# A two-layer hybrid decoder on one core: attention in another order, evacuations of one product put off, some transposes later

## The chip, the cores and the metric

The kernel runs on one core of one Trainium2 chip. The metric is the device time of one execution in microseconds. A core has a matrix engine (PE, with its weight loads shown apart as PEld), a vector engine (DVE), an activation engine (ACT), a general engine (POOL, GpSimd) and a queue engine (SP) that issues most of the transfers here. Each engine takes its own instructions in order, and they meet through semaphores.

## The reference, cut to what matters

One sequence of 1024 tokens, 1024 wide, goes through two layers in float32. Layer 0 mixes tokens with a gated linear recurrence (HGRN2, 8 heads of 128), layer 1 with sliding-window attention (window 128, 16 query heads of 64, 4 key/value heads, a learned sink per head and a shared relative-position bias). Each layer ends in a gated FFN with a causal convolution of width 3, and every sub-layer is `x <- LayerNorm(alpha * x + sublayer(x))`. The attention, which the change rewrites most, is

```python
logits = einsum('bntgrd,bnsgd->bngrts', q, kk) * scale + bias      # query block n against key blocks n-1, n
logits = where(mask, logits, -inf)                                 # 0 <= t - s < 128
m = maximum(logits.max(-1), sink)
p = exp(logits - m[..., None])
denom = p.sum(-1) + exp(sink - m)
o = einsum('bngrts,bnsgd->bntgrd', p, vv) / denom
```

Of the 256 keys that a query block sees, row t uses exactly 128: keys s > t of the block before and keys s <= t of its own block. The kernel therefore folds both halves into one 128 x 128 tile of probabilities per head and block.

## The kernel before, in words

**Precision.** A float32 product is made of three matmuls on high and low parts (`mm3`, L190 to L194): `split` writes the high part with an ACT copy (L218, a CAST) and the low part with a DVE subtraction (`low_part`, L166). A low part can be put off: when `split` gets a list, the subtraction is appended to it and runs when `make_lows` (L1376) empties the list. Smaller products run as plain float32 matmuls (`mm32`, L197) and transposes go through PE (`tr`, L201).

**Stages.** HGRN2 (to about 510 us), its output projection and the first FFN (to about 1230 us), keys and values, attention (about 1275 to 1470 us), the second output projection and FFN (to the end). The order on PE is the program's everywhere. In HGRN2 and in attention the orders on ACT, DVE and POOL are the program's too (`manual_schedule`); in the FFN stages DVE and ACT follow a planner.

**HGRN2.** A small planner, `Order`, interleaves the recurrence of one head with the projections of the next: `od.t` counts PE's estimated time, and a generator that yields a delay goes on when that time has passed. `norm` (L979) squares the head's output on ACT, takes the root on POOL, scales `og` on DVE (L990), yields `od.behind(0.5, 2.4)`, and then turns `og` by eight PE transposes.

**Output projection and normed rows.** `out_proj` (L299) makes the second half of the rows in the order of row blocks 4 to 7 and 0 to 3. For each, `Up.ln` (L360) normalises the row block on DVE (`ln_affine`: L249, L252), yields 8.0 us of PE time, and then turns the block on PE (L201) for the FFN.

**The FFN's second product.** `Down.product` (L600) computes seven products of the Strassen-Winograd form in the order 1, 2, 5, 6, 7, 3, 4. Each fills four PSUM banks (row blocks tb = 0 to 3); products 1, 5, 7 and 4 use the four banks of `psmm`, products 2, 6 and 3 those of two `psax` tiles, where tb = 0 and tb = 2 are the two halves of one tile, tb = 1 and tb = 3 those of the other. The last five blocks of the sum run bank after bank, and each bank is evacuated (`evacuate`, L582: L589 and L591 on DVE) as soon as its last matmul is issued. Product 3 of the last layer alone holds the evacuation of a bank back until the bank two later is done.

**Attention.** 32 iterations: c = 0 to 7 (a pair of head groups and a head within), bp = 0 to 3 (two query blocks). `attend` (L1279) is a generator with seven steps, and four iterations are in flight. Counted from the iteration n in which a unit starts:

| step | work | engine | in iteration |
|---|---|---|---|
| 1 | scores (L1290), copy of the own block's half to X (L1293) | PE, ACT | n |
| 2 | the other half by predicate (L1297), bias (L1303) | DVE, POOL | n |
| 3 | maximum (L1308, L1311), four exponentials with sums (L1315), the sink's (L1317) | DVE, ACT | n+1 |
| 4 | sum, reciprocal, scaling of X (L1319 to L1321) | DVE | n+1 |
| 5 | four transposes of X into one PSUM bank (L201) | PE | n+2 |
| 6 | two masked multiplications from that bank into W, s <= t and s > t (L1329) | DVE | n+2 |
| 7 | products with V of this block and the one before (L197), copy of the result (L1342) | PE, ACT | n+3 |

The loop (L1408 on) takes one step of each unit in flight: step 1 of the new one, 7 of the oldest, 3, 2, 5, 6, one filler on PE, 4, the split of a finished half of the next q (`q_split`, L1274 on ACT and L1276 on DVE, in every second iteration, bp = 0 and 2), the low parts that wait, and a second filler. A filler is six matmuls of 512 columns: of the next q's projection while c < 7, of the output projection (`out_part`) in c = 7. In the iterations 26 to 31 (`moves`) a finished piece of the attention's result is split into T (`Y_to_T`), its ACT cast at the head of the iteration. After the loop the last three units are taken to their ends by hand, with parts of the output projection between.

Of the kernel before, what the change touches and what calls it, by code (L numbers as in the profile page):

```python
# [10 lines left out]
F32 = mybir.dt.float32  # L11
# [24 lines left out]
def constant_arrays():  # L36
    s = np.arange(P)[:, None]
    t = np.arange(P)[None, :]
    masks = np.zeros((P, 7 * BL + P), np.float32)
    bs, bt = s % BL, np.arange(BL)[None, :]  # L40
    pair = lambda m: (bs // (2 * m) == bt // (2 * m)) & (bs % (2 * m) < m) & (bt % (2 * m) >= m)
    parts = [bs == bt, pair(1), pair(2) & (bs % 4 == 0), pair(2) & (bs % 4 == 1)] + [pair(1 << i) for i in range(2, 5)]
    for i, part in enumerate(parts):
        masks[:, i * BL:(i + 1) * BL] = part
    masks[:, 7 * BL:] = t > s
    tri = np.zeros((P, 2, P), np.float32)
    tri[:, 0] = s <= t
    tri[:, 1] = s > t
# [59 lines left out]
def trunk(ctx: ExitStack, tc: tile.TileContext, a: dict, out: bass.AP):  # L108
# [237 lines left out]
    class Up:  # L346
# [13 lines left out]
        def ln(self, tb):  # L360
            with urgent():
                ln_affine(tb, self.rows, lambda hs: ynd[:, tb, hs], 2 if tb == 3 else 1)
            yield 8.0
            turned = lambda t: (self.rx[2 * t - 4] if t in (2, 3) else Y[:, t, :]).rearrange("p (k t) -> p k t", k=KC)
# [145 lines left out]
    class Down:  # L510
# [89 lines left out]
        def product(self, i, ln):  # L600
# [7 lines left out]
            for k, tb in steps + [(k, tb) for tb in range(4) for k in range(late, H)]:  # L608
# [6 lines left out]
                if k == H - 1:  # L615
                    if i < 2:
                        self.later.append(lambda p=p, tb=tb: self.evacuate(p, tb, banks[tb], ln))
                    elif self.last and p == 3:
                        held.append(tb)
# [30 lines left out]
    with tc.tile_pool(name="t", bufs=1, reuse_waits="tile") as raws, hgrn_pool as hp:  # L650
# [328 lines left out]
        def norm(h, pv, og):  # L979
# [11 lines left out]
            od.vec(1.2)  # L991
            yield od.behind(0.5, 2.4)
            ps = psax()
# [198 lines left out]
    with (tc.tile_pool(name="ta", bufs=1, reuse_waits="tile") as raws,  # L1192
          tc.tile_pool(name="at", bufs=1, reuse_waits="tile") as at):
        raw_tail(raws)
        Kh = at.tile([P, 2, 2, S], F32R, name="Kh")
        tri = at.tile([P, 2, P], F32, name="tri")
        nc.scalar.dma_start(tri, a["tri"])
# [4 lines left out]
        Kl = at.tile([P, 2, S], F32R, name="Kl")  # L1202
        Vt = at.tile([P, NB, 256], F32, name="Vt")
        khl, uv = [], []
        for c in range(2):
# [23 lines left out]
        def v_part(tp):  # L1229
            ps = psmm()  # L1230
            proj_tok(uv, tp, ps)
            nc.scalar.copy(Vt[:, 2 * tp:2 * tp + 2, :], ps.rearrange("p (a b) -> p a b", a=2))

        wq = a["swa_w_q"][0].rearrange("(kc p) (h e) -> p kc h e", p=P, e=64)

        W0 = at.tile([P, 2, 4, P], F32, name="W0")
        bfs = {}
# [41 lines left out]
        def attend(c, bp, q):  # L1279
# [44 lines left out]
            for i in range(4):  # L1324
                tr(pt[:, i * P:(i + 1) * P], X[:, i // 2, i % 2, :])
            yield
            W = W0 if bp % 2 else Y[:, NB - 1, :].rearrange("p (k g s) -> p k g s", k=2, g=4)
            for k in range(2):
                nc.vector.tensor_tensor(W[:, k], pt.rearrange("p (g s) -> p g s", g=4),  # L1329
                                        tri[:, k, :].unsqueeze(1).to_broadcast([P, 4, P]), op=ALU.mult)  # L1330
            yield
            po = psmm()
            for jj in range(2):
                j = 2 * bp + jj
                for e in range(2):
                    kvc = (2 * pp + e) * 64
                    o = po[64 * e:64 * e + 64, jj * P:(jj + 1) * P]
                    mm32(o, Vt[:, j, kvc:kvc + 64], W[:, 0, 2 * e + jj, :], stop=j == 0)
                    if j:
                        mm32(o, Vt[:, j - 1, kvc:kvc + 64], W[:, 1, 2 * e + jj, :], start=False)  # L1340
            if c < 7:
                nc.scalar.copy(Y[:, c, bp * 256:(bp + 1) * 256], po[:, :256])  # L1342
            else:
                ts = slice(bp * 256, (bp + 1) * 256)
                split(T[:, 0, c, ts], T[:, 1, c, ts], po[:, :256], lows)
            yield
# [34 lines left out]
        with tc.manual_schedule(engines={EN.PE, EN.Activation, EN.DVE, EN.Pool}):  # L1381
# [117 lines left out]
```

## Time and profile before

| | |
|---|---|
| median of 3 runs | 2189.2 us (2187.97 to 2191.01) |
| the profiled execution's own time | 2192.32 us |
| span of the profile | 2190.5 us |
| PE busy / its weight loads | 99% / 83% of the span |
| DVE busy | 80% |
| ACT busy | 41% |
| POOL busy | 5% |
| granted TensorE clock, mean | 0.997 |

A busy PE is one with a matmul in flight; the ends of matmuls are modelled, so that short waits between two of them do not show as idle time, and a matmul at a lower clock counts as busy for longer. The two places to look are therefore the waits of PE and the granted clock. A row of a timeline gives the start in us, the length in us, engine, line, operation, out<-in, shapes and count, and in brackets how long the engine was idle before it and what ended that. A row of the windows gives for each engine the busy time and the number of instructions, then the granted clock, the share of the DMA engines and GB/s.

### The profile page before, as it was taken

To read this page: it belongs to the slowest core of one execution; us is meant where nothing else is said; L and a number is where in the kernel's file an instruction comes from. 1 tells how busy PE (TensorE), PEld (TensorE's weight loads), DVE (VectorE), ACT (ScalarE), POOL (GpSimd) and SP (SyncE) were. 2 spreads that over 40 slices of the span, in tenths; PEclk is the share of its full clock that TensorE was granted. 3 is DMA by queue.
4 is the path that set the end of the run, shared out by engine and by line. 5 is a ranking of instruction groups with operands and counts; after the bars stand their busy time and mean duration, and the time that the engine had idled before them with its cause. 6 is when DMAs were issued, how large, how long until landed. Compare 5 with 4: busy or idle time off the path is not lost.

```text
span 2190.5 us, 33214 instructions
## 1 busy us (share of the span) xinstructions
PE 2168.1 (99%) x13188; PEld 1813.6 (83%) x13188; DVE 1762.2 (80%) x2388; ACT 895.3 (41%) x1457; POOL 120.3 (5%) x135
## 2 busy tenths in 40 slices
PE   9999999999999999999999999999999999999998
PEld 8888888998888888888878888878888888888877
DVE  3776666667999988887978568969999988878986
ACT  3233333343444444444433256743544444434430
POOL 1000000000100000000001123211000000000001
PEclk9999999999999999999999999999999999999999
DMA  5654533305223222228854411133223222249662
GB/s 196 231 167 162 183 136 102 97 22 175 98 73 106 87 85 79 77 96 271 281 183 154 126 32 28 32 106 110 93 96 97 77 87 77 84 138 325 229 209 88
DMA packets 229844, 279.05 MB, mean 127 GB/s; under 512 B 29960, under 2 KB 158648, under 8 KB 226872
## 3 DMA queue, kind: packets, MB, share of 16 engines
q1 hardware_dynamic: 228736, 276.53, 38.7%
q8 instruction: 104, 1.70, 0.3%
q14 instruction: 52, 0.43, 0.1%
q10 hardware_dynamic: 856, 0.37, 0.1%
q0 software_dynamic: 96, 0.02, 0.0%
HBM read 213.94 MB, written 62.94 MB: 126 GB/s over the span
## 4 chain that ended last, share of the span: by engine, by line
PE 84%; DVE 9%; DMA 3%; issue 2%; ACT 2%; SPq 0%; POOL 0%; DVEq 0%; ACTq 0%; POOLq 0%
PE psmm L191 18%; PE psmm L193 17%; PE psmm L192 17%; PE psax L191 8%; PE psax L192 8%; PE psax L193 8%; PE psax L197 3%; DVE T L166 2%; PE psax L201 1%; DVE HL L166 1%; PE psmm L201 1%; PE psmm L197 1%; PE psax L1290 1%; DMA R<-bsd 1%; DMA rx<-gd 1%
## 5 line engine op out<-in xcount | busy, mean ns | idle before, releaser
L191 PE MATMUL psmm<-T,HL 128*128 128x512 f32 x768 | 307.4, 400 | 0.0
L192 PE MATMUL psmm<-T,HL 128*128 128x512 f32 x768 | 300.3, 391 | 0.0
L193 PE MATMUL psmm<-T,HL 128*128 128x512 f32 x768 | 300.2, 391 | 0.0
L470 DVE SCALAR_TENSOR_TENSOR Y<-Y,cwt 128x1023 f32<-128x1023 f32 (+1 forms) x176 | 225.1, 1281 | 43.3 <-ACT Y L468 39.9
L218 ACT CAST HL<-rx 128x1024 fp32r<-128x1024 f32 (+1 forms) x151 | 151.0, 1004 | 219.9 <-PE psmm L192 45.0
L191 PE MATMUL psmm<-HL,T 128*128 128x256 f32 (+1 forms) x656 | 198.3, 302 | 0.0
L193 PE MATMUL psmm<-HL,T 128*128 128x256 f32 (+1 forms) x656 | 194.3, 296 | 1.4 <-DVE T L166 1.4
L192 PE MATMUL psmm<-HL,T 128*128 128x256 f32 (+1 forms) x656 | 194.0, 296 | 0.0
L166 DVE TENSOR_TENSOR HL<-rx,HL 128x1024 fp32r<-128x1024 f32 (+1 forms) x151 | 174.4, 1161 | 19.1 <-ACT HL L218 18.9
L193 PEld LDWEIGHTS psmm<-T,HL 128*128 128x128 f32 x768 | 144.2, 188 | 31.3
L191 PEld LDWEIGHTS psmm<-T,HL 128*128 128x128 f32 x768 | 144.3, 188 | 30.6 <-issue 0.4
L192 PEld LDWEIGHTS psmm<-T,HL 128*128 128x128 f32 x768 | 144.4, 188 | 28.2
L468 ACT ACTIVATE Y<-Y,cwt 128x1024 f32<-128x1024 f32 x88 | 108.8, 1238 | 103.6 <-DVE Y L457 96.0
L192 PE MATMUL psax<-T,HL 128*128 128x512 f32 x352 | 137.8, 391 | 0.0
L191 PE MATMUL psax<-T,HL 128*128 128x512 f32 x352 | 137.7, 391 | 0.0
L193 PE MATMUL psax<-T,HL 128*128 128x512 f32 x352 | 137.4, 390 | 0.0
L191 PEld LDWEIGHTS psmm<-HL,T 128*128 128x128 f32 x656 | 125.3, 191 | 6.2 <-issue 2.5
L193 PEld LDWEIGHTS psmm<-HL,T 128*128 128x128 f32 x656 | 125.3, 191 | 5.2 <-DVE T L166 2.1
L192 PEld LDWEIGHTS psmm<-HL,T 128*128 128x128 f32 x656 | 125.4, 191 | 3.3
L240 POOL TENSOR_TENSOR rs<-rs,nhalf 128x1 f32<-128x1 f32 x32 | 45.6, 1424 | 1420.4 <-DVE rs L239 1420.4
L166 DVE TENSOR_TENSOR HL<-raw,HL 128x1024 fp32r<-128x1024 f32 x51 | 62.4, 1225 | 66.7 <-ACT HL L173 66.4
L191 PEld LDWEIGHTS psax<-T,HL 128*128 128x128 f32 x352 | 66.1, 188 | 14.6
(293 smaller groups left out, 5087.0 us busy)
## 6 DMA issues: line engine op xcount, KB each, us to landing
rx<-in_ffn_w_in_dram SPq DMA_DIRECT2D x136, 256.0 KB, 3.5
rx<-gd SPq DMA_DIRECT2D x118, 256.0 KB, 3.4
Y<-in_ffn_w_out_dram SPq DMA_DIRECT2D x44, 512.0 KB, 5.8
bsd<-Y SPq DMA_DIRECT2D x22, 1024.0 KB, 4.7
gd<-Y SPq DMA_DIRECT2D x44, 512.0 KB, 2.6
rx<-in_ffn_w_out_dram SPq DMA_DIRECT2D x54, 256.0 KB, 3.7
R<-bsd SPq DMA_DIRECT2D x44, 256.0 KB, 4.6
Y<-in_ffn_w_in_dram SPq DMA_DIRECT2D x40, 256.0 KB, 3.0
```

The lines of the kernel that those rows point to most:

```text
L166: make = lambda e: e.tensor_tensor(lo, src, hi.bitcast(F32), op=ALU.subtract)
L191: nc.tensor.matmul(ps, st(0), mv(0), start=start, stop=False)
L192: nc.tensor.matmul(ps, st(0), mv(1), start=False, stop=False)
L193: nc.tensor.matmul(ps, st(1), mv(0), start=False, stop=stop)
L197: nc.tensor.matmul(ps, lhsT, rhs, start=start, stop=stop, **kw)
L201: nc.tensor.transpose(ps, src, ident)
L218: nc.scalar.copy(hi, src)
L240: nc.gpsimd.tensor_tensor(rs, rs, nhalf, op=ALU.pow)
L468: nc.scalar.activation(c, u, AF.Identity, bias=cwt[:, l, 3, ci:ci + 1], scale=cwt[:, l, 2, ci:ci + 1])
L470: nc.vector.scalar_tensor_tensor(c[:, sh:], u[:, :S - sh], cwt[:, l, 2 - sh, ci:ci + 1], c[:, sh:], op0=ALU.mult, op1=ALU.add)
L1290: nc.tensor.matmul(pv[:, e, jj, lo:], q[bp // 2][es, e, qs], Kl[es, pp, ks] if low else Kh[:, pp, e, ks], start=not low and jj == 0, stop= ...
```

## The change

Five edits. (1) In attention the probabilities of step 5 are no longer masked twice: ACT copies the whole transposed tile from PSUM back to X, DVE makes only the part s <= t as W, and the product becomes V[j-1] against X plus (V[j] - V[j-1]) against W, with the difference dV made once by POOL beside the values. (2) The loop's order: scores, products of the oldest unit, the ACT cast of `Y_to_T` (it stood ahead of the scores), step 3, step 2, the waiting low parts (they stood behind `q_split`), the first filler, step 5, step 4, step 6, `q_split`, the second filler. (3) The tail after the loop is written anew. (4) Product 6 of both FFNs holds its evacuations back as product 3 of the last does. (5) The row blocks 4 to 7 are turned 10 instead of 8 us behind their normalisation, and the heads' `og` is turned at least 3.4 instead of 2.4 us after its scaling (the last head's still 2.4).

```diff
-            yield 8.0
+            yield 10.0 if tb > 3 else 8.0
             turned = lambda t: (self.rx[2 * t - 4] if t in (2, 3) else Y[:, t, :]).rearrange("p (k t) -> p k t", k=KC)
...
-                    elif self.last and p == 3:
+                    elif p == 6 or self.last and p == 3:
                         held.append(tb)
                         if tb > 1:
                             self.evacuate(p, held.pop(0), banks[tb - 2], ln)
...
-            yield od.behind(0.5, 2.4)
+            yield od.behind(1.2, 2.4 if h == NH - 1 else 3.4)
...
+        dV = at.tile([P, NB - 1, 256], F32, name="dV")
...
             nc.scalar.copy(Vt[:, 2 * tp:2 * tp + 2, :], ps.rearrange("p (a b) -> p a b", a=2))
+            b0 = max(2 * tp, 1)
+            nc.gpsimd.tensor_tensor(dV[:, b0 - 1:2 * tp + 1, :], Vt[:, b0:2 * tp + 2, :], Vt[:, b0 - 1:2 * tp + 1, :],
+                                    op=ALU.subtract)
...
             yield
-            W = W0 if bp % 2 else Y[:, NB - 1, :].rearrange("p (k g s) -> p k g s", k=2, g=4)
-            for k in range(2):
-                nc.vector.tensor_tensor(W[:, k], pt.rearrange("p (g s) -> p g s", g=4),
-                                        tri[:, k, :].unsqueeze(1).to_broadcast([P, 4, P]), op=ALU.mult)
+            X = X.rearrange("p e j s -> p (e j) s")
+            nc.scalar.copy(X, pt.rearrange("p (g s) -> p g s", g=4))
+            W = Y[:, NB - 1, :].rearrange("p (k g s) -> p k g s", k=2, g=4)[:, bp % 2]
+            nc.vector.tensor_tensor(W, pt.rearrange("p (g s) -> p g s", g=4),
+                                    tri.unsqueeze(1).to_broadcast([P, 4, P]), op=ALU.mult)
             yield
...
-                    mm32(o, Vt[:, j, kvc:kvc + 64], W[:, 0, 2 * e + jj, :], stop=j == 0)
                     if j:
-                        mm32(o, Vt[:, j - 1, kvc:kvc + 64], W[:, 1, 2 * e + jj, :], start=False)
+                        mm32(o, Vt[:, j - 1, kvc:kvc + 64], X[:, 2 * e + jj, :], stop=False)
+                    mm32(o, dV[:, j - 1, kvc:kvc + 64] if j else Vt[:, 0, kvc:kvc + 64], W[:, 2 * e + jj, :], start=j == 0)
...
-                split(T[:, 0, c, ts], T[:, 1, c, ts], po[:, :256], lows)
+                first = []
+                split(T[:, 0, c, ts], T[:, 1, c, ts], po[:, :256], first)
+                lows[:0] = first
...
+                    stage(it)
+                    stage(prev[0])
                     if 4 * c + bp in moves:
                         Y_to_T(*moves[4 * c + bp], lows)
-                    stage(it)
-                    stage(prev[0])
                     stage(prev[2])
                     stage(it)
+                    make_lows()
+                    stage(fill)
                     stage(prev[1])
+                    stage(prev[2])
                     stage(prev[1])
-                    stage(fill)
-                    stage(prev[2])
                     while done:
                         q_split(*done.pop(0))
-                    make_lows()
...
             next(a31)
             next(a29)
+            Y_to_T(4, 6, 4, 8, lows)
+            make_lows()
+            out_part(begun[2], us, 2, range(4))
             next(a30)
+            next(a31)
             next(a30)
+            out_part(begun[2], us, 2, range(4, 7))
+            out_part(begun[3], us, 3, range(2))
+            next(a30)
+            next(a31)
+            next(a31)
+            Y_to_T(6, 7, 4, 8, lows)
             make_lows()
-            out_part(begun[2], us, 2, range(6))
+            out_part(begun[3], us, 3, range(2, 7))
             next(a31)
             make_lows()
-            next(a30)
-            out_part(begun[2], us, 2, [6])
-            next(a31)
-            next(a31)
-            make_lows()
-            Y_to_T(4, 7, 4, 8)
-            out_part(begun[3], us, 3, range(4))
-            next(a31)
-            make_lows()
-            out_part(begun[3], us, 3, range(4, 7))
             for tb in range(4, 6):
```

More of the change, by code (lines that the diff above doesn't have):

```diff
@@ L45, in constant_arrays @@
     masks[:, 7 * BL:] = t > s
-    tri = np.zeros((P, 2, P), np.float32)
-    tri[:, 0] = s <= t
-    tri[:, 1] = s > t
+    tri = (s <= t).astype(np.float32)
     onehot = np.zeros((32, 2 * P), np.float32)
@@ L1195, in trunk @@
         Kh = at.tile([P, 2, 2, S], F32R, name="Kh")
-        tri = at.tile([P, 2, P], F32, name="tri")
+        tri = at.tile([P, P], F32, name="tri")
         nc.scalar.dma_start(tri, a["tri"])
@@ L1232, in v_part @@
             nc.scalar.copy(Vt[:, 2 * tp:2 * tp + 2, :], ps.rearrange("p (a b) -> p a b", a=2))
+            b0 = max(2 * tp, 1)
+            nc.gpsimd.tensor_tensor(dV[:, b0 - 1:2 * tp + 1, :], Vt[:, b0:2 * tp + 2, :], Vt[:, b0 - 1:2 * tp + 1, :],
+                                    op=ALU.subtract)
         wq = a["swa_w_q"][0].rearrange("(kc p) (h e) -> p kc h e", p=P, e=64)
-        W0 = at.tile([P, 2, 4, P], F32, name="W0")
         bfs = {}
```

## The prediction

> **What bounds the kernel now.** The page first, then PE's waits, longest in total first (microseconds in total, times, longest).
>
> ```profile
> span 2190.5 us, 33214 instructions
> PE 2168.1 (99%) x13188; PEld 1813.6 (83%) x13188; DVE 1762.2 (80%) x2388; ACT 895.3 (41%) x1457; POOL 120.3 (5%) x135
> ...
> PE psax L191 <- DVE Y L591: 3.2, 2, 1.7
> ...
> PE psmm L197 <- DVE W L1329: 2.4, 3, 1.4
> PE psmm L201 <- DVE T L166: 1.5, 1, 1.5
> PE psmm L193 <- DVE T L166: 1.4, 2, 1.1
> PE psmm L201 <- DVE Y L252: 1.0, 1, 1.0
> ...
> PE psax L201 <- DVE og L990: 0.6, 1, 0.6
> PE psmm L201 <- DVE X L1321: 0.6, 3, 0.2
> ```
>
> PE sets the time, so only its waits and its clock can be won. Three waits lie outside attention: 3.2 us for evacuations in the two FFNs, 1.0 for a normed row (L252), 0.6 for `og`. The other four are attention's, 2.4 + 1.5 + 1.4 + 0.6 = 5.9 us. The windows, third, show where (busy us of PE, PEld, DVE, ACT, POOL with counts; then the clock).
>
> ```profile
> 1445.00:1450.00 5.00, 3.86 (x31) 2.77 (x29) 4.86 (x12) 3.63 (x14) 1.62 (x2) 1.00 0.37 152
> 1450.00:1455.00 5.00, 3.00 (x23) 2.62 (x24) 4.58 (x11) 1.24 (x7) 0.54 (x1) 0.70 0.24 48
> ...
> 1453.10:1458.80 5.70, 5.68 (x16) 4.64 (x17) 3.44 (x9) 2.00 (x10) 0.00 (x0) 0.50 0.57 187
> ```
>
> At attention's end PE idles 1.1 and 2.0 of 5 us while DVE is busy for 4.9 and 4.6 of them, so DVE is the engine that PE waits for; then 5.70 us run at half clock, which costs 5.70 x 0.5 = 2.9 us. So attention holds 5.9 + 2.9 = 8.8 us.
>
> **The three edits outside attention.** Product 6: PE waits in the middle of a sum.
>
> ```profile
> 1121.98 0.50 PE L191 MATMUL psax<-T 128*128 128x512 f32 x1 [1.74 <-DVE Y L591]
> ...
> 1117.77 0.69 DVE L565 TENSOR_TENSOR rx<-rx,R 128x512 f32<-128x512 f32 x1 [1.76 <-DMA rx<-gd]
> 1118.38 1.22 DVE L166 TENSOR_TENSOR T<-rx,T 128x1024 fp32r<-128x1024 f32 x1
> ...
> 1120.11 1.21 DVE L589 TENSOR_TENSOR Y<-Y,psax 128x1024 f32<-128x1024 f32 x1
> ...
> 1448.41 0.39 PE L192 MATMUL psmm<-HL,T 128*128 128x512 f32 x1
> 1448.63 0.40 PE L193 MATMUL psmm<-HL,T 128*128 128x512 f32 x1
> ```
>
> The first matmul of the third bank waits for the evacuation of the first, which lies in the same `psax` tile; that evacuation came late because DVE stood 1.76 us at a transfer. Held back, it is issued behind the third bank's last matmul, and nothing on PE is left to wait: -3.2 us for both layers. The four evacuations then follow one another, some 4 x (1.21 + 0.69, a 128x512 operation as at 1117.77) = 7.6 us of DVE, beside the next product, which fills the four `psmm` banks with 4 x 11 x 3 = 132 matmuls, 0.22 us apart (the last two rows), 29 us. That cover hides them; without it (the next operands' low parts late behind them on DVE) up to the same 3.2 us come back. I take all of it.
>
> The normed rows: 2 us more before the turn of blocks 4 to 7 exceed the 1.0 us; the rows turned are wanted only after the other four blocks' matmuls. -1.0, no DMA moves. `og`: +1 us exceeds the 0.6 us wait: -0.6. Its PSUM tile is one of two of `psax`, taken later; at worst each of seven heads waits as long as the one that waited, 7 x 0.6 = +4.2. I take -0.6, since PE shows no other wait for `og` and the planner puts other matmuls there. Sum: -4.8.
>
> **Attention, operations.** No DMA is added or moved: the loads of q's weights and of the output weights stay where they were, behind the split of q. Per iteration one DVE masked multiplication of 128x512 goes, one ACT copy of that size comes. Their prices, and a pair of engines at one bank:
>
> ```profile
> 571.53 0.59 ACT L375 COPY Y<-psmm 128x512 f32<-128x512 f32 x1 [1.22 <-DVE T L166]
> ...
> L1303 POOL TENSOR_TENSOR X<-X,bf x32: 1263/1292/1302, 1280.2 to 1449.3; 128x512 f32<-128x512 f32 x32
> ...
> L1321 DVE TENSOR_TENSOR X<-X,dn x32: 691/691/695, 1284.8 to 1456.6; 128x512 f32<-128x512 f32 x32
> ...
> L1329 DVE TENSOR_TENSOR W<-psmm,tri x32: 673/680/691, 1297.4 to 1463.6; 128x512 f32<-128x512 f32 x32
> ```
>
> A masked multiplication is 0.68, a copy 0.59. PE's matmuls stay the same in number and shape. POOL's four differences, estimated at the 1.29 of its 128x512 addition, lie before the loop or in its second iteration, on an engine 5% busy; at worst the last delays one bias, 0 to +1.3. I take 0. ACT and DVE now read the same PSUM bank, and in the first row an ACT copy waited 1.22 us for DVE's read of its bank. So W will wait for the copy, and behind W on DVE stand the split of q and the next maximum, for which the exponentials wait.
>
> **Attention, order.** Here I see a new loop. Step 6 now stands behind step 4 on DVE, and step 4 waits for this iteration's exponentials; W goes into PE's products at the head of the next iteration, ACT copies their result before the next exponentials. Its length from rows of one stretch:
>
> ```profile
> 1373.52 1.14 PE L197 MATMUL psmm<-W,Vt 128*64 128x128 f32 x16
> ...
> 1374.70 0.37 ACT L1342 COPY Y<-psmm 128x256 f32<-128x256 f32 x1 [0.48 <-PE psmm L197]
> 1374.97 0.40 ACT L1315 ACTIVATE X<-X,nm 128x128 f32<-128x128 f32 x1
> ...
> 1376.52 0.20 ACT L1317 ACTIVATE se<-se 128x4 f32<-128x4 f32 x1
> ...
> 1377.16 0.69 DVE L1321 TENSOR_TENSOR X<-X,dn 128x512 f32<-128x512 f32 x1
> ...
> 1449.03 1.28 DVE L1329 TENSOR_TENSOR W<-psmm,tri 128x512 f32<-128x512 f32 x2
> ...
> 1450.45 1.11 PE L197 MATMUL psmm<-W,Vt 128*64 128x128 f32 x16 [1.43 <-DVE W L1329]
> ...
> 1367.25 1.41 DVE L1276 SCALAR_TENSOR_TENSOR q<-psmm,q 64x512 fp32r<-64x512 f32 x2
> ...
> 1369.68 0.40 ACT L1315 ACTIVATE X<-X,nm 128x128 f32<-128x128 f32 x1
> ```
>
> Products to exponentials: 1374.97 - 1373.52 = 1.45. Exponentials to scaling: 1377.16 - 1374.97 = 2.19. Scaling 0.69, W 0.68, to PE 1450.45 - 1449.03 - 1.28 = 0.14; the two matmuls against X, 2/16 of 1.14 = 0.14, run ahead: 1.37. Loop: 5.01 us. PE's own iterations, by the starts of the products:
>
> ```profile
> 1341.91 1.07 PE psmm L197 x16
> ...
> 1352.55 1.07 PE psmm L197 x16
> ...
> 1362.95 1.07 PE psmm L197 x16
> ```
>
> Two take 10.64 or 10.40. A loop of 5.01 fits in. But in every second iteration the split of q stands behind W: from the start of those two DVE operations to the next exponentials 1369.68 - 1367.25 = 2.43. Exponentials to exponentials is then 2.19 + 0.69 + 0.68 + 2.43 = 5.99, and a pair 1.45 + 5.99 + 2.19 + 1.37 = 11.00, against 10.64 or 10.40: PE waits 0.36 or 0.60, and 0.20 or 0.44 if two operations overlap by 0.08 (the rows at 1117.77 and 1118.38: 0.61 apart, the first 0.69 long). Six pairs of each sort before iteration 26: 3.8 to 5.8; from below, 0 if the X half runs further ahead. I take **+4.5**, nearer to the overlapped row. The ACT copy starts by 1376.52 + 0.1, 1.65 behind the first exponential, ends 2.24 behind it, and W starts 2.88 behind it: cover 0.64, and the low parts (1.22) run beside the exponentials.
>
> Iterations 26 to 31: the cast of `Y_to_T` now stands between that copy and the exponentials.
>
> ```profile
> 1427.93 1.03 ACT L218 CAST T<-Y 128x1024 fp32r<-128x1024 f32 x1
> 1428.87 0.57 ACT L1293 COPY X<-psax 128x512 f32<-128x512 f32 x1
> ...
> 1414.61 0.63 PE L1290 MATMUL psax<-Kh,q 128*128 128x256 f32 x4
> ...
> 1444.92 0.63 PE L1290 MATMUL psax<-Kh,q 128*128 128x256 f32 x4
> ...
> 1445.91 0.93 PE L197 MATMUL psmm<-Y,Vt 128*64 128x128 f32 x12
> ...
> 1453.12 1.09 PE L201 MATMUL psmm<-ident,X 128*128 128x128 f32 x4 [1.55 <-DVE T L166]
> ```
>
> It adds 0.94, loop 5.95; one of five casts is half as long: 4 x 5.95 + 5.48 = 29.3, with low parts that run past the exponentials (0 to 0.6) 29.3 to 29.9, against 1444.92 - 1414.61 = 30.3 now. I take **-0.6**.
>
> The tail: from the last products in the loop PE has the work from 1445.91 to 1448.63 + 0.22, 2.94 us, before the next products, and the loop is 5.95 to 6.3: PE idles 3.0 to 3.4. Now it idles 1.43 + 1.55 = 3.0 in two pieces; the second (a bank not yet free) goes (12 of the output projection's matmuls now stand between the products and those transposes). So +0.2 in waits. The clock: now it falls during those two pieces. A single piece of 3.2 us is at least as idle, and I expect the fall again, 3 in 4. It then costs 2.9 to 3.4, since the slow stretch now began in the second idle piece (clock 0.70 from 1450 to 1455 and 0.50 from 1453.1, so some 6.8 us in all) and would lie wholly in work: +0.3. Together **+0.5**; without the fall -2.7.
>
> On that clock the Trainium skill has a rule (TensorE: Matmul & The Clock Gate, section "Why this matters for your kernels"): no gaps over about 3 us between bursts, or one idle window halves the rate. The rows differ: gaps of 1.43 and 1.55 sufficed. By the page's rule the new gap stands right at the limit, which makes the sum 0 or 3.4 there.
>
> The wait of 1.1 for a low part of T (L193 <- L166) also goes, since low parts are now made half an iteration earlier; it lies within the 30.3. Sum: +4.5 - 0.6 + 0.5 = +4.4 in attention, -4.8 outside: **-0.4**, span 2190.1. The profiled execution was 2192.3 with 1.8 around its span, 3.1 above the median; on the median's scale 2189.2 - 0.4 = **2188.8**.
>
> **Rivals.** *The loop fits*: if it is shorter by 0.3 per pass (the X half hides W), the pairs come to 10.4 and PE waits nowhere but in the tail, 5.0 - 2.94 = 2.1, with the clock kept. For it: DVE loses 0.68 us per iteration where PE waited for it. Against: the rows' sum. 8.8 - 2.1 = 6.7 plus 4.8: 2177.7. *The loop binds harder (slower)*: W held by the copy of the same bank. It decides from a copy that ends 0.64 later than worked out, as the transposes now stand behind six matmuls; with W 0.25 later still, each of 12 pairs pays twice, 6.0, and each late iteration once, 1.5: 2188.8 + 7.5 = 2196.3. For it: the row at 571.53; against: the cover. *The held evacuations give nothing*: product 7's operands wait behind them; +3.2, 2192.0; against: 29 us of cover.
>
> **How the numbers follow.** A measurement tells about 0.2% (4.4 us) from no change. Forecast 0.45, the loop fits 0.28, binds harder 0.19, evacuations give nothing 0.08. The forecast's own range is 2185 to 2193. Faster: 0.28 and 0.05 of the forecast (clock kept, short pairs), 0.33; slower: 0.19 and 0.03, 0.22; same 0.45. The range takes in both neighbours' prices: 2177 to 2197.
>
> **What would show it.** Right: PE rows at L197 in every second iteration with 0.2 to 0.6 of idle time ended by W (L1329's successor), iterations 26 to 31 near 5.95, one idle piece near 3 us ahead of a window at clock 0.5, and no wait on L591, L252 or `og`. Wrong: pairs that stay at 10.4 and 10.64, or waits for the ACT copy.

## The result, and the profile after

The changed kernel takes 2203.9 us (median of 6 runs, 2202.1 to 2205.6), the kernel before took 2189.7 beside it (6 runs): 1.0068 times, with an interval of 1.0058 to 1.0079. The forecast was 2188.8 in a range of 2177 to 2197, and 2196.3 was its slow rival. Both were too fast. The profiled execution of the changed kernel took 2203.71 with a span of 2201.9, so it lies at its median; the one of before lay 2.6 above its own (2189.7), so the two spans differ by 11.4 only.

The first lines of the page after, and PE's waits (us in total, times, longest). Line numbers are two lower than before in the helpers and the FFN, and one to three higher in attention: the matmuls against W are now L195, W itself L1332, its PSUM copy L1330, the bias addition L1304, the sum `dn` L1320.

```profile
span 2201.9 us, 33216 instructions
PE 2173.6 (99%) x13188; PEld 1815.4 (82%) x13188; DVE 1754.7 (80%) x2357; ACT 910.8 (41%) x1490; POOL 133.3 (6%) x139
...
PE psmm L195 <- DVE Y L1332: 12.0, 17, 1.6
...
PE psmm L191 <- DVE HL L164: 1.7, 2, 0.9
PE psmm L195 <- ACT X L1330: 1.5, 1, 1.5
PE psax L195 <- DVE Ab L856: 1.1, 1, 1.1
...
PE psax L189 <- DVE Y L589: 0.4, 1, 0.4
```

The same 13188 matmuls, 31 fewer DVE instructions, and yet PE waits 12.0 us in 17 places for W, where it waited 2.4 in three. The 3.2 for evacuations at product 6 (was L591, now L589) is gone; the 0.4 on L589 belongs to another product, at 1060.52. The waits for L252 and for `og` are gone too. Outside attention two waits are new: low parts of weights (HL, 1.7) and `Ab` of HGRN2's first head (1.1).

How the loss is spread shows in the starts of the scores, one row for each iteration, counted from 0: iteration 0 of the kernel before, then iterations 0, 26 and 31 after.

```profile
1276.00 0.62 PE L1290 MATMUL psax<-Kh,q 128*128 128x128 f32 x4
```

```profile
1274.69 0.62 PE L1291 MATMUL psax<-Kh,q 128*128 128x128 f32 x4
...
1426.19 0.64 PE L1291 MATMUL psax<-Kh,q 128*128 128x256 f32 x4
...
1460.06 0.63 PE L1291 MATMUL psax<-Kh,q 128*128 128x256 f32 x4
```

In us, worked out from these rows and from those of before (1276.0, 1414.61, 1444.92):

| | before | after | difference | forecast |
|---|---|---|---|---|
| up to the first scores | 1276.0 | 1274.7 | -1.3 | -4.8, with the second FFN |
| iterations 0 to 25 | 138.6 | 151.5 | **+12.9** | +4.5 |
| iterations 26 to 31 | 30.3 | 33.9 | **+3.6** | -0.6 |
| from the last scores to a matmul of the output projection (the 10401st; it starts at 1543.73 before, 1555.72 after) | 98.8 | 95.7 | -3.1 | +0.5 |
| from there to the end | | | -0.6 | |

The steady middle repeats every four iterations (bp = 0 to 3): 5.30, 5.32, 5.32, 5.10 us before, 5.94, 5.41, 6.52, 5.17 after, 2.0 more for every four. The end of attention in windows (busy us of PE, PEld, DVE, ACT, POOL, then PE's granted clock):

```profile
1440.00:1445.00 5.00, 3.42 (x21) 2.62 (x20) 3.24 (x9) 1.84 (x4) 2.63 (x4) 0.74 0.00 2
1445.00:1450.00 5.00, 5.00 (x38) 3.99 (x36) 4.28 (x8) 3.96 (x14) 0.00 (x0) 0.92 0.00 0
...
1460.00:1465.00 5.00, 4.09 (x31) 2.86 (x30) 4.55 (x9) 3.46 (x13) 1.28 (x1) 1.00 0.00 0
1465.00:1470.00 5.00, 3.46 (x25) 2.70 (x26) 2.93 (x9) 2.75 (x13) 0.00 (x0) 1.00 0.61 210
```

The clock fell here too, but behind a gap within the last iterations and not in the tail:

```profile
1442.04 0.32 PE L195 MATMUL psmm<-Y,dV 128*64 128x128 f32 x1 [1.58 <-DVE Y L1332]
...
1465.61 0.43 PE L195 MATMUL psmm<-X,Vt 128*64 128x128 f32 x2 [1.48 <-ACT X L1330]
1466.98 0.32 PE L195 MATMUL psmm<-Y,dV 128*64 128x128 f32 x1 [0.93 <-DVE Y L1332]
```

The windows at 0.74 and 0.92 hold 5 x 0.26 + 5 x 0.08 = 1.7 us of lost clock, 3.4 us at half speed, where the stretch before was some 6.8 long. At the last two rows the clock stays at 1.00.

**What the middle waits for.** Rows ahead of PE's wait in one of the 6.52 us iterations, without PE's other work:

```profile
1376.46 0.40 ACT L1316 ACTIVATE X<-X,nm 128x128 f32<-128x128 f32 x1 [0.44 <-DVE nm L1312]
...
1377.07 1.21 DVE L164 TENSOR_TENSOR HL<-raw,HL 128x1024 fp32r<-128x1024 f32 x1
...
1377.32 2.12 POOL L1304 TENSOR_TENSOR X<-X,bf 128x512 f32<-128x512 f32 x1 [0.68 <-DVE X L1298]
...
1378.02 0.19 ACT L1318 ACTIVATE se<-se 128x4 f32<-128x4 f32 x1
1378.11 0.56 ACT L1330 COPY X<-psmm 128x512 f32<-128x512 f32 x1
...
1378.24 1.22 DVE L1320 TENSOR_TENSOR dn<-dn,se 128x4 f32<-128x4 f32 x1
...
1379.49 0.18 DVE L1321 RECIPROCAL dn<-dn 128x4 f32<-128x4 f32 x1
1379.70 0.69 DVE L1322 TENSOR_TENSOR X<-X,dn 128x512 f32<-128x512 f32 x1
...
1380.31 0.68 DVE L1332 TENSOR_TENSOR Y<-psmm,tri 128x512 f32<-128x512 f32 x1
...
1381.05 0.32 PE L195 MATMUL psmm<-Y,dV 128*64 128x128 f32 x1 [0.74 <-DVE Y L1332]
```

Read `dn`: an addition of 128 x 4 numbers lasts 1.22 us. It has no wait ahead of it; it started at 1378.24 and stays on the engine until 1379.46. POOL's bias addition, a different tile of another unit, ends at 1377.32 + 2.12 = 1379.44. And that addition itself lasts 2.12 where it lasts 1.29 otherwise: it began while DVE's low part ran (1377.07 to 1378.28), with 0.96 of it still to come, and lasts 0.83 longer. So POOL seems to stand until DVE's low part is through, and then DVE's sum until POOL's addition is through. Reciprocal, scaling, W and PE's products follow, each at once behind the one ahead, and PE stands 0.74 us. Of the four iterations only one has a low part there; in the 5.94 one this longer stay on the engine, called the hold from here on, is the short one:

```profile
1389.25 1.28 POOL L1304 TENSOR_TENSOR X<-X,bf 128x512 f32<-128x512 f32 x1 [0.67 <-DVE X L1298]
...
1390.17 0.39 DVE L1320 TENSOR_TENSOR dn<-dn,se 128x4 f32<-128x4 f32 x1 [1.06 <-ACT se L1318]
```

0.39, ending with POOL's 1389.25 + 1.28. The kernel before had the same two instructions and, in every second pass, the short hold:

```profile
1370.28 1.27 DVE L1329 TENSOR_TENSOR W<-psmm,tri 128x512 f32<-128x512 f32 x2
1370.52 1.29 POOL L1303 TENSOR_TENSOR X<-X,bf 128x512 f32<-128x512 f32 x1 [0.68 <-DVE X L1297]
1371.47 0.37 DVE L1319 TENSOR_TENSOR dn<-dn,se 128x4 f32<-128x4 f32 x1
...
1375.54 1.29 POOL L1303 TENSOR_TENSOR X<-X,bf 128x512 f32<-128x512 f32 x1 [0.55 <-ACT X L1315]
...
1376.75 0.16 DVE L1319 TENSOR_TENSOR dn<-dn,se 128x4 f32<-128x4 f32 x1 [0.17 <-ACT se L1317]
```

There the two W multiplications (1.27 us, one of their operands in PSUM) ran beside POOL's addition and covered most of it. The Trainium skill states the rule (SBUF — State Buffer, section "Who interferes with whom"): a DVE instruction with two SBUF inputs contends with a GpSimd instruction that reads SBUF, and whichever was issued first keeps the shared ports for the whole instruction. The rows agree in both directions (`dn` behind POOL's addition, POOL's addition behind the low part), and W, with one operand in PSUM, is not held.

This was read from rows. Whether it is the cause, and all of it, is what the runs ask. Five of them (low parts late, no addition, addition unused, copy first, cast first) are one execution each; 21 executions of the kernel before, taken beside two of these, lay between 2187.0 and 2191.4.

### The profile page after: what moved, and what is told of

Its sections match the earlier page's. It is cut to its first block, busy times and chain, and to the rows that moved or that the text cites. A ratio compares the mean times of both kernels' runs of the same rounds, so it can differ in the third digit from the quotient of the medians.

```text
span 2201.9 us, 33216 instructions
## 1 busy us (share of the span) xinstructions
PE 2173.6 (99%) x13188; PEld 1815.4 (82%) x13188; DVE 1754.7 (80%) x2357; ACT 910.8 (41%) x1490; POOL 133.3 (6%) x139
## 4 chain that ended last, share of the span: by engine, by line
PE 85%; DVE 8%; ACT 3%; DMA 2%; issue 2%; SPq 0%; POOL 0%; DVEq 0%; ACTq 0%; POOLq 0%
PE psmm L189 18%; PE psmm L191 17%; PE psmm L190 17%; PE psax L190 9%; PE psax L191 9%; PE psax L189 9%; PE psax L195 3%; ACT X L1316 1%; PE psax L199 1%; PE psmm L195 1%; DVE q L1277 1%; DVE Y L468 1%; DVE HL L164 1%; PE psmm L199 1%; DVE dn L1320 1%
## 5 line engine op out<-in xcount | busy, mean ns | idle before, releaser
L216 ACT CAST HT<-rx 128x1024 fp32r<-128x1024 f32 (+1 forms) x37 | 35.5, 959 | 115.6 <-DVE rx L422 80.8
```

Of the source, the lines that this page charges most:

```text
L216: nc.scalar.copy(hi, src)
```

## The experiments

**The edits outside attention, all three, on the kernel before.**

```diff
-            yield 8.0
+            yield 10.0 if tb > 3 else 8.0
...
-                    elif self.last and p == 3:
+                    elif p == 6 or self.last and p == 3:
...
-            yield od.behind(0.5, 2.4)
+            yield od.behind(1.2, 2.4 if h == NH - 1 else 3.4)
```

> The kernel before with the three edits outside attention alone (product 6 held back, 10 us before the turns, later turns of og). If attention alone made the loss, this one is faster. The sum of the prediction was -4.8 us. PE's instructions, counted off one by one in both traces, give less: +0.6 behind the first head's og, -1.5 at the turns and +1.0 and +1.2 at weights of the two FFNs that are late instead, -1.8 at each held product: about -2 us, 2187.5. If the waits at the weights belong to attention's change and not to the later turns, it is -4.5, 2185.

2187.0 us against 2189.3, ratio 0.9991 (0.9982 to 1.0000). So the loss isn't theirs: the attention part alone is worth about +14.2 + 2.3 = 16.5 us. The waits for weights and for `Ab` are in this run too, at the same two kinds of place, so they come from these edits and not from attention.

**The same arithmetic in the order of before**, with W ahead of ACT's copy (the edit, condensed, against the changed kernel).

```diff
-                    stage(it); stage(prev[0]); Y_to_T; stage(prev[2]); stage(it); make_lows();
-                    stage(fill); stage(prev[1]); stage(prev[2]); stage(prev[1]); q_split
+                    Y_to_T; stage(it); stage(prev[0]); stage(prev[2]); stage(it); stage(prev[1]);
+                    stage(prev[1]); stage(fill); stage(prev[2]); q_split; make_lows()
...
-            nc.scalar.copy(X, pt...)
             nc.vector.tensor_tensor(W, pt..., op=ALU.mult)
+            nc.scalar.copy(X, pt...)
```

> The changed kernel with the loop's order of before (transposes and W ahead of the first filler and of the scaling, low parts last, the cast of Y_to_T at the head), W emitted ahead of ACT's copy of the same bank. Theory order: the loss comes from W standing behind the scaling; first to last scores take 165 to 170 us instead of 185.4 (168.9 before), no waits for W before iteration 22, total 2182 to 2189. Rival arithmetic (the copy and the products with dV are themselves dearer): 180 us or more, total above 2198.

2188.5 us, ratio 0.9996 (0.9987 to 1.0005); the stretch of the scores is 170.5, half a microsecond above what was expected. The middle's intervals are those of before to the hundredth (5.30, 5.32, 5.32, 5.10); `dn` is at most 0.59. PE waits late in attention only, for the copy, which now stands behind the exponentials on ACT (PE's waits, then two rows of the timeline):

```profile
PE psmm L195 <- ACT X L1333: 6.5, 5, 1.8
```

```profile
1427.04 0.56 ACT L1333 COPY X<-psmm 128x512 f32<-128x512 f32 x1
...
1427.66 0.45 PE L195 MATMUL psmm<-X,Vt 128*64 128x128 f32 x4 [1.57 <-ACT X L1333]
```

A masking less, a copy more and the new tail are worth about +1.5 us beside the three other edits (2188.5 against 2187.0, two intervals that overlap). The new order, in which the copy also goes ahead of W again, makes the other 15; how much of that is the copy's place is asked below.

**The low parts back behind the split of q**, so that they don't meet POOL's addition.

```diff
-                    make_lows()
                     stage(fill)
...
                     while done:
                         q_split(*done.pop(0))
+                    make_lows()
```

> The changed kernel with the waiting low parts made behind q's split again, all else as changed. Theory port (a low part beside the exponentials keeps POOL's bias addition, and by it the sum dn, waiting): the scores' intervals behind bp = 1 shrink by 0.6 to 1.0 us, first to last scores 175 to 180 us instead of 185.4, and POOL's addition never takes more than 1.31 us (2.13 in the changed kernel). Theory order alone: low parts matter little, 184 us or more.

2203.5 us, the stretch 185.6: the number of the rival, not of the theory. The hold does get shorter as expected (POOL's addition at most 1.30, `dn` at most 0.59) and the iteration of 6.52 takes 5.71; but 5.94 became 6.33 and 5.17 became 5.41, and iterations 26 to 31 took 34.9. The low part, no longer inside the wait for the exponentials, now stands in the loop between W and the next maximum (L1309), which starts only when it is through:

```profile
1355.28 1.22 DVE L164 TENSOR_TENSOR HL<-raw,HL 128x1024 fp32r<-128x1024 f32 x1
...
1356.41 0.68 DVE L1309 TENSOR_REDUCE nm<-X 128x4 f32<-128x512 f32 x1
```

So this run changes two things at once, and its time tells nothing for or against the hold.

**Without POOL's bias addition** (it leaves out the relative-position bias).

```diff
-            nc.gpsimd.tensor_tensor(X, X, bv..., op=ALU.add)
```

> The changed kernel without POOL's bias addition: the relative-position bias is left out of the logits, nothing else. Theory port: dn never takes more than 0.2 us (median 0.39, up to 1.24 in the changed kernel), each pair of iterations is 0.4 to 1.2 shorter, first to last scores 175 to 179 us. Theory order alone (the exponentials end the chain, not POOL): 184 us or more.

2191.7 us, the stretch of the scores 173.1: lower than either theory said. The four intervals are 5.73, 5.42, 5.48, 5.17, and every `dn` is 0.16. The differences to the changed kernel are where `dn` is long: 6.52 - 5.48 = 1.04 where it was 1.22 in place of 0.16, and 5.94 - 5.73 = 0.21 where it was 0.39. But the run also takes a link out of the chain of data (predicate, addition, maximum).

**The same addition, unused.** POOL does 7/8 of the addition into a scratch tile; nothing reads it and the maximum no longer waits for POOL (so this one too is without the bias).

```diff
+            Z = at.tile([P, 2, 2, 112], mybir.dt.bfloat16, name="Z")
-            nc.gpsimd.tensor_tensor(X, X, bv..., op=ALU.add)
+            nc.gpsimd.tensor_tensor(Z, X[:, :, :, :112], bv[:, :, :112]..., op=ALU.add)
```

> The changed kernel, in which POOL's addition of the bias (7/8 of its elements, written as bf16) goes to a scratch tile that nothing reads: the softmax is computed without the relative-position bias, and the maximum no longer waits for POOL, but POOL is busy at the same places. Theory (DVE's small sum dn is held by POOL's addition while that runs, whoever reads its result): dn has a median of 0.3 to 0.4 us and values up to about 1.2 again, the stretch from the first to the last scores is 182 to 187 us, the span near 2200. Rival (what cost time was the chain of data predicate, addition, maximum): dn about 0.16, the stretch 172 to 175 us, the span near 2190, as without the addition.

2202.5 us, the stretch 185.2, as in the changed kernel (185.4); `dn` has a median of 0.27, a little under the range, and a longest of 1.12. The chain of data is out; an addition that nobody needs costs the same 11 us as the one that is needed. The hold stands in the rows, ending at 1375.75 + 1.95 = 1377.70 and 1376.66 + 1.06 = 1377.72:

```profile
1375.46 1.22 DVE L164 TENSOR_TENSOR HL<-raw,HL 128x1024 fp32r<-128x1024 f32 x1
...
1375.75 1.95 POOL L1305 TENSOR_TENSOR Z<-X,bf 128x448 bf16<-128x448 f32 x1 [0.70 <-DVE X L1298]
...
1376.66 1.06 DVE L1321 TENSOR_TENSOR dn<-dn,se 128x4 f32<-128x4 f32 x1
```

**The addition in two and in four instructions**, the computation whole (the edit for four; for two the inner loop is left out).

```diff
-            nc.gpsimd.tensor_tensor(X, X, bv..., op=ALU.add)
+            for e in range(2):
+                for jj in range(2):
+                    nc.gpsimd.tensor_tensor(X[:, e, jj], X[:, e, jj], bv[:, e], op=ALU.add)
```

> The changed kernel with POOL's bias addition cut in two instructions of 128x256 each; nothing else differs. Theory (dn is held until the POOL instruction then running ends): dn can slip in between the two, so its longest hold falls from 1.24 to about 0.7 us and the first half ends before most dn start; the stretch of the scores falls from 185.4 to 177 to 182 us and the time to some 2196 to 2201. Rivals: if dn waits for POOL's whole burst of work, or if a held dn isn't let in between two back-to-back instructions, dn and the stretch stay (185, 2204), or grow by POOL's second fixed cost; if the middle's loss has nothing to do with dn's duration, the stretch stays too although dn gets shorter.

> As the run with halves, with four instructions of 128x128. Theory: the longest hold of dn falls to some 0.4 to 0.5 us and the median towards 0.3; the stretch falls further, to 175 to 180 us, unless POOL's sum of four instructions grows so much (its 128x4 addition takes 0.20 us, so four may take 1.3 to 2.1 us) that the maximum then waits for POOL. Time 2193 to 2200.

2199.9 us (ratio 1.0051, 1.0035 to 1.0068) and 2197.0 us (1.0036, 1.0023 to 1.0049). The stretch is 182.5 (half a microsecond above the range; the time is within it) and 178.0. In iterations 0 to 25 alone, where the clock of these runs and of the changed kernel does not fall, it is 149.5 and 147.1 against 151.5. POOL works longer for it (4 x 0.46 = 1.84 in place of 1.29), and the kernel still gets faster, since a hold ends with the POOL instruction then running. The sum `dn` in four kernels (least, median, longest ns): before, after, halves, quarters.

```profile
L1319 DVE TENSOR_TENSOR dn<-dn,se x32: 153/350/662, 1284.3 to 1456.2; 128x4 f32<-128x4 f32 x32
```

```profile
L1320 DVE TENSOR_TENSOR dn<-dn,se x32: 150/390/1240, 1283.0 to 1471.9; 128x4 f32<-128x4 f32 x32
```

```profile
L1321 DVE TENSOR_TENSOR dn<-dn,se x32: 155/164/719, 1282.2 to 1467.8; 128x4 f32<-128x4 f32 x32
```

```profile
L1322 DVE TENSOR_TENSOR dn<-dn,se x32: 155/185/424, 1282.5 to 1463.6; 128x4 f32<-128x4 f32 x32
```

What is left is the low part's turn to be held; with halves it lasts 1.67 in place of 1.21, behind the first half:

```profile
1374.18 2.41 POOL L1305 TENSOR_TENSOR X<-X,bf 128x256 f32<-128x256 f32 x2 [0.28 <-DVE X L1298]
1374.32 1.67 DVE L164 TENSOR_TENSOR HL<-raw,HL 128x1024 fp32r<-128x1024 f32 x1
...
1375.91 0.69 DVE L1321 TENSOR_TENSOR dn<-dn,se 128x4 f32<-128x4 f32 x1
```

0.46 more for the low part and 0.53 for `dn` are 0.99; that iteration takes 6.44 where it takes 5.48 without the addition, 0.96 more.

**The changed arithmetic in the old order, with the copy first.** As the second run, but ACT's copy stays ahead of W in the program.

```diff
+            nc.scalar.copy(X, pt...)
             nc.vector.tensor_tensor(W, pt..., op=ALU.mult)
-            nc.scalar.copy(X, pt...)
```

> The changed arithmetic in the order of the kernel before, ACT's copy of the transposed exponentials ahead of DVE's masked product in the program, as in the changed kernel; there it is issued behind the next exponentials on ACT. If two engines' reads of one PSUM bank exclude each other and go in the program's order (the prediction's rule from the row 571.53), W waits for the copy, 1 to 2 us in most iterations, and the stretch is 175 to 190 us. If not, it is 170.5 as in the run where W comes first.

2207.7 us, the stretch 188.4, 18 more than with W first (1.7 of it a second fall of the clock); `dn` is not the cause here (at most 0.29). W waits for the copy of the same bank:

```profile
1372.60 0.56 ACT L1330 COPY X<-psmm 128x512 f32<-128x512 f32 x1
...
1373.19 0.69 DVE L1332 TENSOR_TENSOR Y<-psmm,tri 128x512 f32<-128x512 f32 x1 [1.93 <-ACT X L1330]
```

So the prediction's rule on two readers of a bank holds, and which of them comes first in the program is worth some 16 us in that order of the loop. (The Trainium skill, PSUM — Partial Sum Buffer, "PSUM bank collisions raise a hardware error", asks that two engines be kept apart at a bank by semaphores; the row shows what such a wait can cost, 1.93 us.) In the changed kernel the rule costs the loop nothing: the copy ended at 1378.11 + 0.56 = 1378.67, W began at 1380.31, right behind the scaling, and in all of the first 31 passes W began at least 0.36 behind the copy's end with no idle time in front. Only in the last pass, in the tail, does W wait for the copy.

**The cast of the attention rows back at the head of iterations 26 to 31.**

```diff
+                    if 4 * c + bp in moves:
+                        Y_to_T(*moves[4 * c + bp], lows)
                     stage(it)
                     stage(prev[0])
-                    if 4 * c + bp in moves:
-                        Y_to_T(*moves[4 * c + bp], lows)
```

> The changed kernel with the cast and turn of the attention rows (Y_to_T) back at the head of iterations 26 to 31, ahead of the next scores and of the older pair's products. If the 0.94 us of cast between the products and the maximum was a link of the loop in the last iterations, as the prediction had it, the four intervals from 26 to 30 get shorter by 0.5 to 0.9 us each, and the span falls by 2 to 4 us to about 2199; the middle of attention stays as it was. If the DVE order (dn, scaling, W behind the low parts) is all that counts there, the span stays within 1 us of 2201.9.

2204.0 us, span 2202.1. One interval of the five got shorter by more than 0.2, 5.69 to 5.32. But the hold grew: `dn` went from 0.16 to 0.72, from 0.16 to 0.44 and from 1.00 to 1.25 in three passes there. Whether the cast's 0.94 is a link of the loop therefore isn't settled; taking it out didn't help while the hold is there.

**Each edit outside attention by itself**: the held evacuations, the later turns of the normed rows, the later turn of `og`, each on the kernel before (the first, second and third part of the diff above).

> The kernel before with only the held evacuations of product 6 in both feed-forward stages. The prediction has -3.2 us for it (twice 1.6); the run with the three outer edits showed -1.75 and -1.8 at the two places. So 2185.5 to 2186.5 against 2189.3 for the kernel before. If the gain of the outer edits came from elsewhere, it is within 1 us of the kernel before.

> The kernel before with only the later turns of the normed rows (10.0 in place of 8.0 behind row block 3). The prediction has -1.0 us. The run of the three outer edits showed -1.5 at the turns of the first feed-forward stage and then +1.0 at its first product, where the weights' low part came late. If the late weights come from the later turns: two waits of about 0.8 us on the low part ahead of the first products, and a time within 0.7 us of the kernel before. If they come from another edit: no such waits and about -1.5 to -3 us.

> The kernel before with only the later turns of og (1.2 and 3.4 in place of 0.5 and 2.4). The prediction has -0.6 us, the wait for og gone. In the changed kernel and in every run with this edit so far the og wait is gone and PE waits 1.1 us for Ab of head 0 instead. If that wait comes from this edit, it stands in this run too and PE is 0.5 to 0.7 us later than before at its end; if it comes from another edit, it isn't there and PE is 0.6 us earlier. Either is below what the times can tell, so 2187 to 2191.

| | us | before | ratio |
|---|---|---|---|
| held evacuations | 2185.5 | 2188.5 | 0.9986 (0.9977 to 0.9995) |
| normed rows later | 2189.5 | 2188.5 | 1.0005 (0.9995 to 1.0014) |
| `og` later | 2189.7 | 2188.6 | 1.0006 (0.9997 to 1.0016) |

The evacuations alone give -3.1 us and are the fastest of all these kernels. The four of them run in one burst while product 7 is under way; first and last row in the changed kernel, 7.0 us together:

```profile
1124.43 1.22 DVE L587 TENSOR_TENSOR Y<-Y,psax 128x1024 f32<-128x1024 f32 x1 [0.34 <-PE psax L191]
...
1130.76 0.68 DVE L589 TENSOR_TENSOR Y<-Y,psax 128x512 f32<-128x512 f32 x1
```

The other two give nothing that can be measured. PE's waits in the run with the normed rows, and then in the run with `og`:

```profile
PE psmm L193 <- DVE HL L166: 1.5, 2, 0.8
...
PE psax L191 <- DVE Y L591: 0.5, 2, 0.3
```

```profile
PE psax L197 <- DVE Ab L858: 1.1, 1, 1.1
PE psmm L193 <- DVE HL L166: 0.8, 1, 0.8
```

Each trades its wait for another of the same size: the normed rows' 1.0 (L252) for two of 0.75 at the FFNs' first products, the 0.6 for `og` for 1.1 of `Ab`. The `og` edit brings one of the weights' waits as well, so that wait isn't the normed rows' alone; which DVE work pushes the low part back in each case was not tried. The second row of the first fence tells something on reading one profile: the wait of 3.2 for evacuations that the prediction quoted is 0.5 in this execution of a kernel that still has it (this one execution was the fastest of its ten, 2186.7), and 0.6 in the run with `og`. So the wait differs from one execution to the next, and that the timed runs give 3.1 where one profile had 3.2 is in part luck: their interval runs from about 1 to 5 us.

The stretches of the scores, all in us:

| | iterations 0 to 25 | 26 to 31 | sum |
|---|---|---|---|
| before | 138.6 | 30.3 | 168.9 |
| after | 151.5 | 33.9 | 185.4 |
| old order, W first | 139.1 | 31.4 | 170.5 |
| old order, copy first | 154.7 | 33.7 | 188.4 |
| low parts late | 150.7 | 34.9 | 185.6 |
| cast first | 151.5 | 33.4 | 184.9 |
| addition unused | 151.4 | 33.8 | 185.2 |
| addition in halves | 149.5 | 33.0 | 182.5 |
| addition in quarters | 147.1 | 30.9 | 178.0 |
| no addition | 143.5 | 29.6 | 173.1 |

The profiled executions differ in the clock here. In iterations 26 to 31 the changed kernel, both runs in the old order, the late low parts, the first cast and the unused addition each have 3.4 us at half clock (1.7 us of time); the copy-first run has the same once more in iterations 0 to 25. The others have none in these stretches, so that of the 2.9 us that the halves save 1.7 are the clock.

## Why the prediction was wrong, and where it was right

**The step that failed** is the middle of attention, +4.5, and in it one term: "Exponentials to scaling: 1377.16 - 1374.97 = 2.19". In the changed kernel it measures 1379.70 - 1376.46 = 3.24 in the pass shown, 2.42 in the pass with the short hold, and 2.19 in the other two of every four; without the addition it is 2.19 in every pass of the middle. The term was taken from a pass in which `dn` began at 1376.75, 0.08 before POOL's addition ended (1375.54 + 1.29 = 1376.83), so that nothing was left of the hold. In the middle of before that is every second pass; in the passes between, `dn` takes 0.36 to 0.38. The row 0.37 at 1371.47 in the same stretch, and the median of 0.35 against a least of 0.15 over all 32, show in the trace of before that the term has a part that hangs on POOL. There it was hidden, since W (1.27 us, not held) ran beside the addition. The change moves W behind `dn` and puts the low part ahead of it, so that `dn` meets the whole hold: 0.39 in one iteration of four, 1.22 in another. The prediction costed POOL as "an engine 5% busy" and asked only whether POOL's own results come in time.

The missing term is 151.5 - 143.5 = 8.0 us of the 12.9, and the unused addition (151.4) shows that it is POOL's running and not its result.

**The sum of the loop came out, but in part by luck.** Without the addition iterations 0 to 25 take 143.5, +4.9 against before where the sum said +4.5; four iterations take 21.80, where the sum said 21.04 + 0.64 to 0.96 = 21.7 to 22.0. But the sum had all of it as waits for W and held PE's own iteration fixed. The iteration with bp = 3, in which PE shows no wait in either kernel, takes 5.17 after and 5.10 before: the two fillers now stand apart, and behind the first matmul of a filler the next one starts later (1341.16 to 1341.50, 0.34) than behind the others (1341.50 to 1341.73, 0.23). At 0.07 in each of 24 iterations that is an estimated 1.7 us, which leaves 3.2 for waits. Nor do the pairs share it as forecast: 10.62 became 11.15 and 10.42 became 10.65, where the sum had 0.20 to 0.36 for the first and 0.44 to 0.60 for the second.

**Iterations 26 to 31**, -0.6: without the addition -0.7 (29.6, in intervals of 5.63 to 6.23, on average 5.91 where the sum had 5.95), with it +3.6. Between the two lie 4.3 us. Of these, 3.41 us at half clock are 1.7, and the hold lengthens the term from exponentials to scaling by 1.9 in all; 0.7 is open. The 0.94 for the cast was in the sum as a link of the loop, and the run that moved it left that unsettled. That both sums nearly agree without the addition doesn't show each of their terms.

**The tail**, +0.5: measured -3.1. There is no single idle piece of 3.0 to 3.4; PE stands 1.48 and then 0.93 us (at 1465.61 and 1466.98), probably since the iterations ahead had already paid for the lateness (no run asks it), and the clock didn't fall there. "Without the fall -2.7" was near. Against the run of the three outer edits, which has the old attention and kept its clock (95.96 us for the same piece), it is only -0.3: 2.9 of the 3.1 are the fall of before's profiled execution, not a gain of the new tail.

**Outside attention**, -4.8: measured -2.3 together (0 to -3.9). The evacuations' -3.2 came out as -3.1 alone, nearer than its interval allows to claim; the burst of 7.6 measured 7.0, and the rival "held evacuations give nothing" falls. The normed rows' -1.0 and the -0.6 of `og` were taken from the wait that goes, without asking which DVE work then comes later; both came to nothing.

**The rivals.** *The loop fits* falls: even without the addition the pairs take 11.15 and 10.65, not 10.4. *The loop binds harder* had the right sign and the right shape (W late, paid in the split iterations and again at the end), and its rule on the bank is real, but it isn't the cause: of the cover of 0.64 at least 0.36 was left in every pass of the loop, and W was held by what stands ahead of it on DVE. The sign to watch for, "rows at L197 with 0.2 to 0.6 of idle time ended by W", came larger: 0.74 in the row shown, and 1.6 at most.

**What stays open**: why weights come late after the normed rows' and `og`'s edits; what makes the last 0.7 us of iterations 26 to 31; whether the cast is a link there; and what the new order would take with W ahead of the copy, which no run has.

## What to carry to other kernels

Before a short DVE operation with both operands in SBUF is moved, look at what POOL is doing at its new place: here its price was not its own 0.15 us but the rest of the POOL instruction then running, and a median well above the least duration in the view by tile was the sign that the hold was already there, hidden. Where POOL's work must stay, it can be cut in pieces (4 and 7 us less here), or DVE operations with an operand in PSUM can be put beside it, as the kernel before has it (no run here tries that by itself). And take a loop's terms from the median and the worst pass, not from the one pass that happens to be unhindered.

## What the runs showed of the hardware that was not expected

- The hold goes by instruction: the longest `dn` is 1.24 us with one POOL instruction of 1.29 (2.13 when held itself), 0.72 with two of 0.74 and 0.42 with four of 0.46. It goes both ways: POOL's addition grew from 1.29 to 2.13 behind a low part, and a low part from 1.21 to 1.67 behind POOL's first half.
- In the profiled executions the clock in attention fell to half for 6.8 us, for 3.4, for 3.4 twice, or not at all. Before and the run of the three outer edits have the same two gaps of PE there, 1.43 and 1.55; the four transposes behind the second took 1.09 in before, at half clock, and 0.63 in the other run:

```profile
1448.88 1.12 PE L197 MATMUL psmm<-W,Vt 128*64 128x128 f32 x16 [1.43 <-DVE W L1329]
...
1451.55 0.63 PE L201 MATMUL psmm<-ident,X 128*128 128x128 f32 x4 [1.55 <-DVE T L166]
```

  The fall cost before 2.9 us (98.8 against 96.0 for the same piece). Gaps of that size allow a fall and don't settle it, so a fall read in one profile is no part of a kernel's price that a change can be sure to win back.
